# 64 latent tokens leave the dense expert path for the gathered one; V computed with tokens moving

## The chip, the cores and the metric

One core of a Trainium2 chip runs the program. The time is device microseconds from launch to end. The program is one fully unrolled stream per engine: TensorE (PE, with weight loads PEld), VectorE (DVE), ScalarE (ACT), GpSimd (POOL), and SyncE (SP), which only issues DMAs. DMAs of SP, ACT and POOL share 16 DMA engines.

## What is computed

Two layers over five tiles of 128 tokens: four tiles of latents (512 tokens) and one tile of prompt. A layer has a mixer (four head groups between an input and an output projection) and a retrieval of experts (PEER), both modulated by shifts, scales and gates from a conditioning vector, both closed by a layer norm. The change is in PEER:

```python
sv, si = lax.top_k(sc, 16)                            # 8 heads, 2 halves, 128 keys each
cand = sv[:, :, 0, :, None] + sv[:, :, 1, None, :]    # 16 x 16 sums a head
cv, ci = lax.top_k(cand.reshape(nt, 8, 256), 16)
idx, gate = i1 * 128 + i2, softmax(cv)                # 128 experts of 16384 a token
act = gelu(einsum('thkd,td->thk', u_tab[idx], x))
out = einsum('thk,thkd->td', gate * act, v_tab[idx])
```

## The kernel before

**Two ways through PEER.** The 128 prompt tokens take the *gathered path*: for each of a token's 128 experts one indirect DMA brings 128 rows of 4 KB (one per token, 512 KB), and one DVE instruction makes a dot with the token's hidden row (`gather_u`, line 1047) or adds the row, weighted, to an accumulator (`gather_v`, line 1055). That is 128 + 128 gathers a layer. The 512 latents take the *dense path*: all 16384 experts against all latents, in 128 chunks of 128 experts, with a gate matrix that is zero where a token did not choose the expert.

**U** (`a_chunk`, line 1030). A chunk of 512 KB is loaded on SP's queue, split into a high and a low float32r half (ACT copies, DVE subtracts; POOL in the first 12 chunks), and 24 matmuls of 512 columns (experts stationary, latents moving) make [128 experts, 512 tokens] in one PSUM bank. ACT applies gelu, and the ACT queue writes the block to DRAM (`gad`). Between chunks come the gathers of the prompt, the choice of 16 of 256 candidates (`pick`, line 960: one `top16` of five DVE instructions a head) and `build_gate` (line 991): per latent tile 16 steps, each two one-hot and two product tiles on DVE, 16 small f16 matmuls and two ACT copies, written to DRAM (`Gd`) by the ACT queue. The layer's main loop (lines 1222 to 1236) asks for one gather a chunk and spreads the gate's steps over chunks 4 to 108.

**V** (`v_phase`, line 1069). For a chunk, `prep` loads the hidden block (256 KB), every fourth chunk a gate tile (1 MB), and 512 KB of the second table; DVE multiplies hidden by gate, ACT and DVE split product and table into halves, and then `steps` yields one gather (two on every sixteenth chunk) and, in layer 0, `mods` one modulation block on every second chunk from 6 on. `use` makes 24 matmuls: for each of four token tiles six of 512 columns, product stationary, table moving, so that [tokens, 1024] grows in two PSUM banks a tile and all eight banks are taken:

```python
mm(p0, w[:, 0, ns], vh[:, h0], a, False)
mm(q0, w[:, 0, ns], vh[:, h1], a, False)
```

The last three chunks (`TAIL`) run tile by tile in an order written out by hand, and `close_layer` (line 1137: gate, residual, layer norm, in layer 0 also the next layer's norm and transposes) follows each tile as it is done, under the matmuls of the next.

**Modulation.** A layer's 48 blocks of 128 are dots of weight rows with the conditioning vectors, two DVE instructions a block (`mod_block`, `dot_mod`). Layer 0 makes its own in the opening, its mixers (`late_mods`, blocks 16 to 32), its routing (`route_mods`, 32 to 40) and the end of U (40 to 48); all 48 of layer 1 stand in layer 0's V.

**Order of the work.** Dependencies are tracked by tile. A planner that estimates each instruction's time orders the instructions of every engine, except where an order is written by hand; engines and queues then run in that order. `issue_after` puts instructions behind a given one. Buffers: four for gathered rows, in U two of them in idle residual tiles; ten split halves, six hidden blocks, two gate tiles.

Of the kernel before, what the change touches and what calls it, by code (L numbers as in the profile page):

```python
# [73 lines left out]
XLAST = 120  # L74
CS = 32 ** -0.5


def build(tc, nc, I, O, dbg=None):
# [311 lines left out]
    def late_mods(P, o3):  # L390
# [7 lines left out]
        for b in range(16, MID):  # L398
            pt = P.tile([128, 2, 2], F32, name="mp", bufs=4)
            for i in range(2):  # L400
                c = slice(i * 512, (i + 1) * 512)
                w = P.tile([128, 640], F32, name="e", bufs=EB)[:, :512]
                load(w, I["wmodT"][0, b, :, c])
# [8 lines left out]
            V.tensor_add(modT[0][:, :, b:b + 1], pt[:, :, 0:1], pt[:, :, 1:2])  # L412
            finish_mod(0, b, b + 1, modT[0][:, :, b:b + 1])
# [40 lines left out]
    def mixers(l, P, acc, w):  # L454
# [112 lines left out]
        mods = late_mods(P, o3) if l == 0 else iter(())  # L567
# [300 lines left out]
    def out_and_route(l, P, hn, sv, si):  # L868
# [7 lines left out]
        def norm2(n):  # L876
            post_norm(P, n, [part[:, n, 0:1], part[:, n, 1:2]], lg, lb, part[:, n, 2:3])
            k4 = [P.tile([128, D], F32, name="k4", bufs=3) for _ in range(2)]
            normalise(n, k4[0], part[:, n, 2:3])
            nc.scalar.dma_start(xm[l][n], xs[n])  # L880
            modulate_T(n, l, 24, 32, k4[0], (p1(), p1()), k4[1])
            hf_ = k4[1].rearrange("p (a b) -> p a b", a=8)
            if n == PT:
                ps = p2()
                for k in range(8):
                    T.transpose(ps[:, k * 128:(k + 1) * 128], hf_[:, k, :], ident)
                S.activation(hn, ps, AF.Copy)

        def route_mods():
# [6 lines left out]
            for b in range(MID, 40):  # L896
                t = P.tile([128, 4, 2, 128], F32, name="sc", bufs=3).rearrange("p a b c -> p (a b c)")
                load(t, I["wmodT"][0, b])
                dot_mod(t, 0, b, sB, P.tile([128, D], BF16, name="jk", bufs=1))
                yield  # L900

        mods = route_mods() if l == 0 else iter(())
# [57 lines left out]
    def pick(P, n, sv, si, i1, i2, gt):  # L960
# [4 lines left out]
        cand = P.tile([128, 8, 16, 16], F32, name="cand", bufs=1)  # L965
        G.tensor_tensor(cand, sv[:, :, 0, :, None].to_broadcast([128, 8, 16, 16]),
                        sv[:, :, 1, None, :].to_broadcast([128, 8, 16, 16]), OP.add)
        for h in range(8):
            top16(cand[:, h].rearrange("p a b -> p (a b)"), cv[:, h, :], ci[:, h, :])
# [3 lines left out]
        V.tensor_single_scalar(ab[:, 1], ci, 15, OP.bitwise_and)  # L973
        abf = P.tile([128, 2, 8, 16], F32, name="abf", bufs=1)
        V.tensor_copy(abf, ab)
        for j, dst in ((0, i1), (1, i2)):
# [14 lines left out]
    def build_gate(P, n, Gd, i1, i2, gt):  # L991
# [3 lines left out]
        i16 = P.tile([128, 2, 128], F16, name="i16", bufs=2)  # L995
        V.tensor_copy(i16, ps[:, :256].rearrange("p (a b) -> p a b", a=2))
        gT = P.tile([128, 2, 128], F32, name="gT", bufs=1)
        g16 = P.tile([128, 2, 128], F16, name="g16", bufs=2)
# [10 lines left out]
        for u in range(4):  # L1009
# [20 lines left out]
    def a_chunk(Q, l, c):  # L1030
# [7 lines left out]
        for k in range(8):  # L1038
            ks = slice(k * 128, (k + 1) * 128)
            mm(ps, uh[:, ks], Hhi[:, k, 0:512], k == 0, False)  # L1040
            mm(ps, uh[:, ks], Hlo[:, k, 0:512], False, False)
            mm(ps, ul[:, ks], Hhi[:, k, 0:512], False, k == 7)
        ga = Q.tile([128, 512], F32, name="ga", bufs=2)
        S.activation(ga, ps, AF.Gelu_apprx_tanh)  # L1044
        return ga

    def gather_u(P, l, idx, hn, dots):
        for k in range(128):
            t = P.tile([128, D], F32, name="gth", bufs=2) if k % 4 < 2 else x_tile(3 + k % 2)
            G.indirect_dma_start(out=t, out_offset=None, in_=I["u"],  # L1050
                                 in_offset=bass.IndirectOffsetOnAxis(ap=idx[:, k:k + 1], axis=0))
            V.scalar_tensor_tensor(t, t, 1.0, hn, op0=OP.mult, op1=OP.mult, accum_out=dots[:, k:k + 1])  # L1052
            yield

    def gather_v(P, l, idx, gt, dots, accp):
        bufs = GV
        S.activation(dots, dots, AF.Gelu_apprx_tanh)
        V.tensor_mul(dots, dots, gt)
        for k in range(128):
            t = P.tile([128, D], F32, name="gth", bufs=bufs)  # L1060
            G.indirect_dma_start(out=t, out_offset=None, in_=I["v"],  # L1061
                                 in_offset=bass.IndirectOffsetOnAxis(ap=idx[:, k:k + 1], axis=0))
            if k == 0:
                V.tensor_scalar(accp, t, dots[:, 0:1], None, op0=OP.mult)
            else:
                V.scalar_tensor_tensor(accp, t, dots[:, k:k + 1], accp, op0=OP.mult, op1=OP.add)  # L1066
            yield

    def v_phase(l, P, pv, Gd, gad, steps, mods, finish):
        ws, gt, lows = {}, {}, []  # L1070

        def load_gate(g):
            gt[g] = P.tile([128, 16, GLD, 32], F32, name="gate", bufs=2)
# [3 lines left out]
        def prep(c):  # L1077
            ga = P.tile([128, 512], F32, name="gr", bufs=6)
# [8 lines left out]
            w = P.tile([128, 2, 512], F32R, name="whl", bufs=4)  # L1087
# [13 lines left out]
        def use(c, n):  # L1101
            w, vh, vl = ws[c]
            ns = slice(n * 128, (n + 1) * 128)
            p0, q0 = pv[n]
            a, z = c == 0, c == NCH - 1
            h0, h1 = slice(0, 512), slice(512, 1024)
            mm(p0, w[:, 0, ns], vh[:, h0], a, False)
            mm(q0, w[:, 0, ns], vh[:, h1], a, False)
            mm(p0, w[:, 0, ns], vl[:, h0], False, False)
            mm(q0, w[:, 0, ns], vl[:, h1], False, False)  # L1110
            mm(p0, w[:, 1, ns], vh[:, h0], False, z)
            mm(q0, w[:, 1, ns], vh[:, h1], False, z)
# [5 lines left out]
        for c in range(NCH - TAIL):  # L1118
# [3 lines left out]
            for n in range(NL):  # L1122
                use(c, n)
# [6 lines left out]
        with tc.manual_schedule(engines={E.PE, E.DVE, E.Activation, E.Pool}):  # L1130
            for i in range(NL + 2):
                for n in {0: (0,), 1: (1,), 2: (2, 3)}.get(i, ()):
                    for c in range(NCH - TAIL, NCH):
                        use(c, n)
                finish(i)

    def close_layer(l, P, n, f, g2, lg, lb):
        t = P.tile([128, D], F32, name="wm", bufs=2)
        if len(f) == 2:
            for h in range(2):  # L1140
                hs = slice(h * 512, (h + 1) * 512)
                V.tensor_mul(t[:, hs], f[h], g2[:, hs])
        else:
            V.tensor_mul(t, f[0], g2)
        yield
        V.scalar_tensor_tensor(xs[n], xs[n], ALPHA, t, op0=OP.mult, op1=OP.add, accum_out=xsum[:, n, 0:1])
        c = sum_coefs(xs[n], [xsum[:, n, 0:1]], P.tile([128, D], BF16, name="jk", bufs=1))
# [14 lines left out]
    for l in range(DEPTH):  # L1162
# [8 lines left out]
        with tc.tile_pool(name=f"q{l}", bufs=1) as Q:  # L1171
            accp = Q.tile([128, D], F32, name="accp")
            A = tc.alloc_tile_pool(name=f"a{l}", bufs=1)
            hn = A.tile([128, D], F32, name="hn")
            gp = Q.tile([128, 128], F32, name="gp")
# [3 lines left out]
            Gd = dram.tile([16, 2, 128, 64 * 32], F32, name=f"Gd{l}")  # L1179
            gad = [dram.tile([128, 512], F32, name=f"gad{l}_{c}") for c in range(NCH)]  # L1180
            with tc.tile_pool(name=f"t{l}", bufs=1) as TP:
# [4 lines left out]
                with tc.tile_pool(name=f"r{l}", bufs=1) as R:  # L1186
                    out_and_route(l, R, hn, sv, si)
                with tc.tile_pool(name=f"tt{l}", bufs=1) as R:
# [12 lines left out]
                    def gates():  # L1201
                        for n in range(NL):
                            nxt = start_pick(n + 1) if n < NL - 1 else iter(())
# [7 lines left out]
                    for n in (PT, 0):  # L1211
# [8 lines left out]
                    steps = gather_u(A, l, idx, hn, dots)  # L1220
                    bg = gates()
                    for c in range(ASPLIT):
                        nc.scalar.dma_start(gad[c], a_chunk(A, l, c))
                        with tc.issue_after(pace[0].ins):
                            next(steps, None)
                        if c >= T0:
                            for _ in range((c + 1 - T0) * 64 // (T1 - T0) - (c - T0) * 64 // (T1 - T0)):
                                next(bg, None)
                    for _ in bg:
                        pass  # L1230
# [140 lines left out]
```

## Time and profile before

| | us |
|---|---|
| median of 3 runs | 4023.82 (4019.87 to 4028.7) |
| profiled execution | 4019.37 |
| its span | 4017.6 |
| PE busy | 3791.2 (94%) |
| DVE busy | 3068.7 (76%) |
| ACT busy | 1435.9 (36%) |
| POOL busy | 1218.5 (30%) |
| moved by DMA | 934.02 MB, 232 GB/s |

Busy time is the union of an engine's instructions. A matmul's end is modelled and matmuls overlap, so PE's pace is better read from the distance of their starts. The DMA share is the mean busy share of 16 engines. The shares of the whole span hide that the stages differ; the rows below are taken by stage.

### The profile page before, as it was taken

Reading aid. Unit: us, or ns where it says so; the run is one execution under the profiler, and the core shown is the slowest. Engines: PE = TensorE matmul, PEld = TensorE weight load, DVE = VectorE, ACT = ScalarE, POOL = GpSimd, SP = SyncE. Lnnn points to the kernel's source line nnn. Section 1 sums busy time; section 2 is a strip of 40 time slices with the busy share of each in tenths; the row PEclk is TensorE's granted clock in tenths of the full one; section 3 lists DMA queues with packets and bytes.
Section 4 is the critical chain, followed back from the end, with each engine's and each line's share of the span. In section 5 each row is a group of like instructions: output and inputs, shape, how many; then the busy total and the mean of one; then the engine's idle time right before and its main releaser. Section 6 shows DMA issues by size and latency. Waiting matters only on the chain. (4 is left out here: it accounts for less than half of the span.)

```text
span 4017.6 us, 52309 instructions
## 1 busy us (share of the span) xinstructions
PE 3791.2 (94%) x18606; PEld 3091.6 (77%) x18606; DVE 3068.7 (76%) x5984; ACT 1435.9 (36%) x2201; POOL 1218.5 (30%) x946
## 2 busy tenths in 40 slices
PE   6799999999999799999999999999999979999998
PEld 5577777777888688888877778777788868888886
DVE  6867799999766588988765659999986537778545
ACT  5443532333333222222344553323343322222222
POOL 5412445442111222322141243553211113343100
PEclk7899999999999899999999999999999989999999
DMA  6223248777888899999831132677788869999763
GB/s 224 79 71 118 84 139 280 251 256 272 292 263 299 298 350 346 342 343 344 261 103 52 58 106 91 237 262 246 243 307 275 263 223 341 348 340 345 251 195 104
DMA packets 405623, 934.02 MB, mean 232 GB/s; under 512 B 32624, under 2 KB 166896, under 8 KB 397168
## 3 DMA queue, kind: packets, MB, share of 16 engines
q1 hardware_dynamic: 280656, 517.34, 39.4%
q0 software_dynamic: 73728, 268.47, 19.0%
q10 hardware_dynamic: 50976, 144.87, 9.7%
q8 instruction: 146, 2.39, 0.2%
q14 instruction: 117, 0.96, 0.1%
HBM read 785.06 MB, written 145.49 MB: 232 GB/s over the span
## 5 line engine op out<-in xcount | busy, mean ns | idle before, releaser
L83 PE MATMUL pa<-Hhi,hl 128*128 128x512 f32 x4096 | 1318.7, 400 | 11.6 <-ACT ga L1044 11.5
L83 PE MATMUL p<-hl,whl 128*128 128x512 f32 x4608 | 1089.3, 390 | 0.0
L83 PEld LDWEIGHTS p<-hl,whl 128*128 128x128 f32 x4608 | 867.5, 188 | 180.3
L83 PEld LDWEIGHTS pa<-Hhi,hl 128*128 128x128 f32 x4096 | 778.9, 191 | 181.5 <-ACT ga L1044 13.9
L83 PE MATMUL pa<-Hlo,hl 128*128 128x512 f32 x2048 | 815.0, 398 | 0.0
L199 ACT ACTIVATE hl<-x 128x1024 fp32r<-128x1024 f32 x284 | 301.3, 1061 | 960.2 <-PE p L83 578.1
L1061 POOL DMA_INDIRECT gth<-v,idx x256 | 361.0, 1410 | 825.2 <-DVE accp L1066 593.6
L199 ACT ACTIVATE hl<-raw 128x1024 fp32r<-128x1024 f32 x292 | 309.0, 1059 | 775.5 <-PE pa L83 373.7
L200 DVE TENSOR_TENSOR hl<-x,hl 128x1024 fp32r<-128x1024 f32 x272 | 345.3, 1270 | 265.6 <-ACT hl L199 260.6
L200 DVE TENSOR_TENSOR hl<-raw,hl 128x1024 fp32r<-128x1024 f32 x246 | 331.2, 1347 | 238.3 <-ACT hl L199 236.2
L83 PEld LDWEIGHTS pa<-Hlo,hl 128*128 128x128 f32 x2048 | 391.3, 191 | 81.5
L83 PE MATMUL pa<-hl,Hhi 128*128 128x512 f32 x1232 | 438.5, 424 | 7.6 <-DVE gtmp L914 2.8
L83 PE MATMUL pa<-hl,whl 128*128 128x512 f32 x1536 | 391.7, 390 | 43.5 <-DMA gr<-gad 22.6
L83 PEld LDWEIGHTS pa<-hl,whl 128*128 128x128 f32 x1536 | 289.2, 188 | 104.2 <-issue 23.0
L1066 DVE SCALAR_TENSOR_TENSOR accp<-gth,dots,accp 128x1024 f32<-128x1024 f32 x254 | 325.3, 1281 | 4.5 <-DMA gth<-v,idx 2.7
L1050 POOL DMA_INDIRECT gth<-u,idx x128 | 165.9, 1296 | 462.9 <-DVE gth L1052 404.9
L1050 POOL DMA_INDIRECT x<-u,idx x128 | 168.9, 1320 | 448.7 <-DVE x L1052 425.6
L83 PEld LDWEIGHTS pa<-hl,Hhi 128*128 128x128 f32 x1232 | 235.4, 196 | 54.9 <-DVE gtmp L914 3.7
L83 PE MATMUL pa<-hl,Hlo 128*128 128x512 f32 x616 | 260.6, 423 | 14.3 <-POOL Hlo L200 10.5
L1006 DVE TENSOR_TENSOR M<-E,g 128x1024 f16<-128x1024 f16 x256 | 189.3, 771 | 58.7 <-PE p L83 57.7
L1024 ACT ACTIVATE stg<-p 128x512 f32<-128x512 f32 x256 | 138.9, 597 | 233.8 <-PE p L83 153.2
L1085 DVE TENSOR_TENSOR gr<-gr,gate 128x512 f32<-128x512 f32 x256 | 175.2, 685 | 24.7 <-DMA gate<-Gd 24.7
(339 smaller groups left out, 4635.6 us busy)
## 6 DMA issues: line engine op xcount, KB each, us to landing
x<-v SPq DMA_DIRECT2D x158, 512.0 KB
raw<-uT SPq DMA_DIRECT2D x130, 512.0 KB
gad<-ga ACTq DMA_DIRECT2D x256, 256.0 KB
Gd<-stg ACTq DMA_DIRECT2D x64, 1024.0 KB
gr<-gad SPq DMA_DIRECT2D x256, 256.0 KB
gate<-Gd SPq DMA_DIRECT2D x64, 1024.0 KB
x<-uT SPq DMA_DIRECT2D x126, 512.0 KB
raw<-v SPq DMA_DIRECT2D x98, 512.0 KB
```

Source lines behind the costliest of these rows:

```text
L83: return T.matmul(out, l, r, start=start, stop=stop, skip_group_check=True)
L199: S.activation(hi, src, AF.Copy)
L200: return (eng or V).tensor_sub(lo, src, hi.bitcast(F32))
L1006: V.tensor_tensor(out, src, col.rearrange("p (q r) -> p q r", r=2)[:, :, None, :].to_broadcast(shape), op)
L1024: S.activation(st[a][:, :, b * 8:(b + 1) * 8], v[:, a], AF.Copy, scale=1.0 / GSCALE)
L1050: G.indirect_dma_start(out=t, out_offset=None, in_=I["u"], in_offset=bass.IndirectOffsetOnAxis(ap=idx[:, k:k + 1], axis=0))
L1061: G.indirect_dma_start(out=t, out_offset=None, in_=I["v"], in_offset=bass.IndirectOffsetOnAxis(ap=idx[:, k:k + 1], axis=0))
L1066: V.scalar_tensor_tensor(accp, t, dots[:, k:k + 1], accp, op0=OP.mult, op1=OP.add)
L1085: V.tensor_mul(ga.rearrange("p (u t) -> p u t", t=32), ga.rearrange("p (u t) -> p u t", t=32), gt[c // GLD][:, :, c % GLD, :])
```

## The change

A tile of latents is cut: the last 64 tokens of tile 3 (`GS`; `R0` = 64 is their first row in the tile) join the gathered path, and the dense path keeps `DN` = 448.

- *Gathered path.* The 64 tokens' 128 experts are laid out as 128 rows by 64 columns (`PARTS` = 2 halves of 64 on the partitions), so they add 64 gathers to U and 64 to V, ahead of the prompt's. Index and gate slices go over the ACT queue into `idx2` and `gp2`; the hidden rows of the tokens are turned in routing, written to `hxd` and loaded twice into `hn2`. In V, the second half's sums are moved by one DMA and added. U asks for 192 gathers over 128 chunks, V for 194 steps over 118 chunks.
- *Dense path.* U's matmuls, gelu, hidden block, gate product and its halves have 448 columns; tile 3 has 8 gate steps instead of 16. Tiles are taken in the order 3, 0, 1, 2.
- *V turned round.* A chunk's table halves are stationary by blocks of 128 columns, the product moves: eight blocks of three matmuls with 448 columns, one PSUM bank a block. At the layer's end each block is scaled by the gate's column into `fT`, and each tile is turned back by eight transposes before it closes.
- *Pick.* Of 256 candidate sums a head, 112 are kept (first four keys with all 16, the other 12 with four), on two POOL instructions; a few small instructions recover the index pair.
- *Modulation.* Layer 1 makes blocks 16 to 48 where layer 0 makes them; layer 0's V keeps 16 of its blocks, one on every sixth chunk.
- *Buffers.* Hidden blocks and gate tiles move to a pool opened before U's last 16 chunks.

The core of the diff:

```diff
+TILES = (3, 0, 1, 2)
+GS = 64
+PARTS = 128 // GS
+R0 = 128 - GS
+DN = 512 - GS
+VEND = 118
+VSTEPS = 128 + GS + PARTS
@@ a_chunk
+            mm(ps[:, :DN], uh[:, ks], Hhi[:, k, :DN], k == 0, False)
...
@@ gather_u
+        for idx, hn, dots, cols in groups:
+            for k in range(cols):
+                t = P.tile([128, D], F32, name="gth", bufs=2) if g % 4 < 2 else x_tile(3 + g % 2)
...
@@ gather_v
+            if cols == GS:
+                for j in range(PARTS - 1):
+                    t = P.tile([128, D], F32, name="gth", bufs=GV)
+                    nc.scalar.dma_start(t[R0:], acc[j * GS:(j + 1) * GS])
+                    V.tensor_add(acc[R0:], acc[R0:], t[R0:])
+                    yield
+                V.tensor_mul(acc[R0:], acc[R0:], g2[R0:])
@@ v_phase
-                next(steps, None)
-                if c % 16 == 15:
+                for _ in range(2 * (c == 0) + (c + 1) * VSTEPS // VEND - c * VSTEPS // VEND):
                     next(steps, None)
-                if c >= MOD0 and (c - MOD0) % 2 == 0:
+                if c >= MOD0 and (c - MOD0) % 6 == 0:
                     next(mods, None)
+        def use(c, b):
+            mm(pv[b], vh[:, bs], w[:, 0], c == 0, False)
+            mm(pv[b], vh[:, bs], w[:, 1], False, False)
+            mm(pv[b], vl[:, bs], w[:, 0], False, c == NCH - 1)
...
+            for b in range(8):
+                for c in range(NCH - TAIL, NCH):
+                    use(c, b)
...
+                if b % 2:
+                    V.tensor_scalar(fT[b], pv[b], g, None, op0=OP.mult)
+                else:
+                    S.activation(fT[b], pv[b], AF.Copy, scale=g)
             for i in range(NL + 2):
                 finish(i)
@@ close_layer
+            for b in range(8):
+                o = f[b * len(f) // 8][:m, b * 128 % (1024 // len(f)):][:, :128]
+                T.transpose(o, fT[b][:, n * 128:n * 128 + m], ident)
@@ build_gate
-        for u in range(4):
+        for u in range(R0 // 32 if n == NL - 1 else 4):
@@ pick
-        cand = P.tile([128, 8, 16, 16], F32, name="cand", bufs=1)
+        cand = P.tile([128, 8, 256], F32, name="cand", bufs=1)[:, :, :112]
+        for a0, a1, nb in ((0, 4, 16), (4, 16, 4)):
...
@@ main loop
-                        next(steps, None)
+                            for _ in range((c + 1) * (128 + GS) // NCH - c * (128 + GS) // NCH):
+                                next(steps, None)
...
+            H = tc.alloc_tile_pool(name=f"h{l}", bufs=1, side="right")
             with tc.tile_pool(name=f"ta{l}", bufs=1) as R:
-                mods = mod_steps(R, [(0, b) for b in range(40, 48)], 4) if l == 0 else iter(())
+                mods = mod_steps(R, [(l, b) for b in range(40, 48)], 2)
...
-                        mod_steps(R, [(1, b) for b in range(48)], 2) if l == 0 else iter(()), finish)
+                        mod_steps(R, [(1, b) for b in range(16)], 2) if l == 0 else iter(()), finish)
```

## Rows read from the trace of the kernel before

**Rows 1.** By stage: us, PE, PEld, DVE, ACT, POOL busy, clock, DMA, GB/s.
```profile
512.00:1329.00 817.00, 781.66 (x4094) 633.18 (x4092) 683.22 (x1318) 288.44 (x409) 259.44 (x150) 0.98 0.74 254
1329.00:1350.70 21.70, 0.58 (x2) 0.51 (x3) 2.72 (x5) 3.65 (x4) 4.68 (x5) 0.56 0.97 311
1350.70:2049.50 698.80, 698.80 (x3079) 578.66 (x3078) 589.24 (x792) 209.95 (x271) 188.99 (x135) 1.00 0.92 319
2049.50:2306.00 256.50, 240.55 (x1373) 193.29 (x1372) 158.02 (x406) 131.07 (x286) 78.14 (x126) 0.97 0.20 65
2306.00:2466.00 160.00, 154.31 (x722) 126.19 (x721) 110.39 (x489) 74.72 (x111) 64.57 (x42) 0.98 0.31 98
2466.00:3283.40 817.40, 784.85 (x4103) 635.86 (x4101) 670.48 (x1292) 282.79 (x404) 249.24 (x150) 0.98 0.73 248
...
3304.00:4002.00 698.00, 697.82 (x3071) 577.50 (x3069) 476.47 (x530) 200.39 (x256) 176.42 (x130) 1.00 0.83 280
```

**Rows 2.** Chain of waits, V of layer 1: start us, us, what.
```profile
3720.31 4.08 PE p L83 x18
3725.75 4.08 PE p L83 x18
```

**Rows 3.** Busy time in two stretches of U of layer 0.
```profile
700.00:900.00 200.00, 184.88 (x958) 147.71 (x958) 200.00 (x361) 70.18 (x100) 82.19 (x42) 0.97 0.73 248
...
1200.00:1329.00 129.00, 127.51 (x588) 104.03 (x587) 69.22 (x103) 44.42 (x57) 18.65 (x15) 1.00 0.75 265
```

**Rows 4.** Timeline, mixers of layer 0: start us, us, engine, line.
```profile
145.52 0.42 PEld L83 LDWEIGHTS p<-x,x 96*128 96x128 f32 x2
145.75 0.45 PE L83 MATMUL p<-x,x 96*128 96x320 f32 x2
...
146.04 0.40 PE L83 MATMUL pa<-hl,Hhi 128*128 128x512 f32 x1
```

**Rows 5.** Groups by form, V of layer 1: busy us, mean ns, idle.
```profile
L1066 DVE SCALAR_TENSOR_TENSOR accp<-gth,dots,accp 128x1024 f32<-128x1024 f32 x99 | 126.8, 1281 | 3.9 <-DMA gth<-v,idx 2.7
L200 DVE TENSOR_TENSOR hl<-x,hl 128x1024 fp32r<-128x1024 f32 x41 | 50.2, 1225 | 39.2 <-ACT hl L199 39.0
...
L1085 DVE TENSOR_TENSOR gr<-gr,gate 128x512 f32<-128x512 f32 x65 | 44.5, 685 | 0.0
```

**Rows 6.** Groups by form, whole span.
```profile
L1006 DVE TENSOR_TENSOR M<-E,g 128x1024 f16<-128x1024 f16 x256 | 189.3, 771 | 58.7 <-PE p L83 57.7
...
L410 DVE SCALAR_TENSOR_TENSOR o<-e,o 128x512 bf16<-128x512 f32 x48 | 36.5, 761 | 3.2 <-DMA e<-wmodT 3.1
...
L418 DVE SCALAR_TENSOR_TENSOR jk<-sc,k 128x1024 bf16<-128x1024 f32 x16 | 19.5, 1220 | 3.1 <-DMA sc<-wmodT 3.1
```

**Rows 7.** DMA view, 3400 to 3650: packets, MB, share of engines; issues.
```profile
q1 hardware_dynamic: 36013, 47.87, 56.5%
q0 software_dynamic: 10279, 37.43, 39.9%
...
gth<-v,idx POOLq DMA_INDIRECT x73
```

**Rows 8.** Line 954: count, ns min/median/max, first, last start.
```profile
L954 DVE MAX8 sv<-sc x160: 274/331/584, 453.4 to 2497.6; 128x8 f32<-128x128 f32 x160
L954 DVE MAX8 cv<-cand x80: 401/406/425, 550.7 to 2812.0; 128x8 f32<-128x256 f32 x80
```

**Rows 9.** Chain of waits, hole of layer 1.
```profile
3285.97 15.38 DMA gate<-Gd
```

**Rows 10.** Timeline, end of layer 1.
```profile
3989.42 12.40 PE L83 MATMUL p<-hl,whl 128*128 128x512 f32 x54
...
4010.77 0.08 DVE L1151 DVE_READ_ACCUMULATOR x<-wm,cf,rowb 128x1 f32 x1
```

**Rows 11.** Waits, 3400 to 3650: us, times, longest.
```profile
POOL gth L1061 <- DVE accp L1066: 140.8, 49, 8.8
...
DVE accp L1066 <- DMA gth<-v,idx: 2.7, 4, 1.2
```

More of the change, by code (lines that the diff above doesn't have):

```diff
@@ L887, in norm2 @@
                 S.activation(hn, ps, AF.Copy)
+            if n == NL - 1:
+                ps = p2()
+                for k in range(8):
+                    T.transpose(ps[:, k * 128:(k + 1) * 128], hf_[:, k, :], ident)
+                hx = P.tile([128, D], F32, name="k4", bufs=3)
+                S.activation(hx, ps, AF.Copy)
+                nc.scalar.dma_start(hxd, hx[R0:])
         def route_mods():
@@ L1039, in a_chunk @@
             ks = slice(k * 128, (k + 1) * 128)
[L1040 to L1044, printed above, removed]
-        return ga
[L1047 to L1067, printed above, removed]
@@ L1070, in v_phase @@
+    def v_phase(l, P, H, pv, fT, Gd, gad, steps, mods, finish):
         ws, gt, lows = {}, {}, []
         def load_gate(g):
-            gt[g] = P.tile([128, 16, GLD, 32], F32, name="gate", bufs=2)
+            gt[g] = H.tile([128, DN // 32, GLD, 32], F32, name="gate", bufs=2)
             cc = g * GLD % 64
@@ L1201, in gates @@
                     def gates():
-                        for n in range(NL):
-                            nxt = start_pick(n + 1) if n < NL - 1 else iter(())
+                        for i, n in enumerate(TILES):
+                            nxt = start_pick(TILES[i + 1]) if i < NL - 1 else iter(())
                             for _ in build_gate(R, n, Gd, i1[n], i2[n], gt[n]):
@@ L1219, in build @@
                             show(n)
-                    steps = gather_u(A, l, idx, hn, dots)
+                        else:
+                            idf = R.tile([128, 128], F32, name="sif", bufs=1)
+                            V.scalar_tensor_tensor(idf, i1[n], 128.0, i2[n], op0=OP.mult, op1=OP.add)
+                            V.tensor_scalar(idf, idf, float(l * 16384), None, op0=OP.add)
+                            idr = R.tile([128, 128], I32, name="ab", bufs=1)
+                            V.tensor_copy(idr, idf)
+                            for j in range(PARTS):
+                                ps_, cs_ = slice(j * GS, (j + 1) * GS), slice(j * GS, (j + 1) * GS)
+                                nc.scalar.dma_start(idx2[ps_], idr[R0:, cs_])
+                                nc.scalar.dma_start(gp2[ps_], gt[n][R0:, cs_])
+                    hn2 = R.tile([128, D], F32, name="hn2")
+                    for j in range(PARTS):
+                        load(hn2[j * GS:(j + 1) * GS], hxd)
+                    steps = gather_u(A, l, ((idx2, hn2, dots2, GS), (idx, hn, dots, 128)))
                     bg = gates()
@@ L1235, in build @@
                     with tc.issue_after(pace[0].ins):
-                        next(steps, None)
+                        for _ in range((c + 1) * (128 + GS) // NCH - c * (128 + GS) // NCH):
+                            next(steps, None)
                     next(mods, None)
@@ L1243, in build @@
                 wide = [p2(), p2()]
-                pv = [(pacc(), pacc()), (p1(), p1())] + [(t[:, :512], t[:, 512:]) for t in wide]
+                pv = [t[:, h * 512:h * 512 + DN] for t in wide for h in range(2)]
+                pv += [t[:, :DN] for t in (p1(), p1(), pacc(), pacc())]
+                acc2 = R.tile([128, D], F32, name="acc2")
+                fT = []
                 if dbg and "f" in dbg:
```

140 lines of the change are left out of this document (90 added, 50 removed).

## The prediction

> **What bounds the kernel now.** The first view to read is the table by stage [rows 1]. A layer is a mixer and routing part, then U (chunks of the first expert table against the latents), a hole, and V (the gated chunks back to tokens). U takes 817 us a layer, V 698; the four together are 3031 of the 4017.6 us, with PE busy 96% of U and all of V. [...] So V is PE's. What the reader is to see beside it: DVE is busy 589 of 699 us in layer 0's V, and the DMA engines 0.92 and 0.83 of the two V stages. In U, DVE is busy 200.0 of 200 us at 700 to 900, and PE is nearly full later, 127.5 of 129 at 1200 to 1329 [rows 3]: DVE sets the pace first, PE at the end.
>
> **The change, part by part.**
>
> *Columns.* Each of the 3072 matmuls of a U stage, and of a V stage, moves 448 columns instead of 512. Is a shorter matmul quicker, when each has a weight load shown as 0.21 us? Two neighbouring 320-column matmuls, each with its load, start at 145.75, and the next matmul at 146.04: 145 ns each [rows 4]. So the load is hidden. (226.7 - 145) / 192 is 0.4255 ns a column, and 448 columns cost 199.5 ns. PE saves 27.2 ns x 3072 = 84 us in each of the four stages, if nothing else is late. A V chunk needs 24 x 199.5 ns = 4.79 us of PE, U 782 - 84 = 698 us (its gate matmuls left whole, though an eighth goes).
>
> *V, on DVE.* By chunk: the gate product, and the low half of it that takes as long, shrink by an eighth from 0.685 to 0.60 each; the low half of the table stays 1.225; gathers come at 194 steps over 118 chunks, 1.64 x 1.281 = 2.10 [rows 5]. Sum 4.53 us, under PE's 4.79. In layer 0 a modulation block, two dots of 1.22 us [rows 6] and some small work, 2.8 together, follows every sixth chunk, 0.47 a chunk: 5.0, a little over PE. Before, 48 such blocks stood there, now 16.
>
> *V, transfers.* The DMA view of 3400 to 3650 has 56.5% of 250 us for the loads of 46 chunks (250 / 5.44), 3.07 us of all 16 engines a chunk, and 39.9% for 73 gathers, 1.366 us each [rows 7]. The gate and the hidden block, half of a chunk's bytes, shrink by an eighth: 2.88. With 1.64 gathers: 2.88 + 2.24 = 5.12 us a chunk. This is the term that decides: for 118 chunks the transfers become the longest, over PE's 4.79, where before 3.07 + 1.07 x 1.366 = 4.53 stood under PE's 5.44. In layer 1 I take 5.15: 118 x 5.15 + 10 x 4.79 = 656 us against 698, **-42**. In layer 0 the 16 blocks load 512 KB each, as a gather does, and DVE is nearer: 5.30, so 673, **-26**. Bounds for each stage: 613 (128 x 4.79, PE's alone) and 698 plus some 30, if DVE, whose instructions go in order, stands behind late gathers.
>
> [...]
>
> *U.* DVE's 683 us [rows 1] change so. 64 more dots of 1.22 and a read: +83. Of 64 gate steps 8 go, each four instructions of 0.77 [rows 6]: -25. The candidates shrink from 256 columns to 112; the maximum over 256 takes 0.406, over 128 at best 0.274 [rows 8], so 40 heads x 5 instructions x 0.13 = -26. Index arithmetic in five picks and one more index tile: +12. Together +44: 727. Transfers: 0.74 x 817 = 605, and 64 gathers x 1.366: 692 (the ACT queue's smaller writes left out). So three resources stand at 698, 727 and 692. Before, the stage took 817 for PE's 782, 4.5% over its longest. With three so close I take 7% over the longest: 778, **-39** a layer, -78. Bounds: 727 (DVE never idle, -90) and 840 (+23, if the backlog of 700 to 900 grows and PE stands behind it). The eight modulation blocks that the end of layer 1's U gets, 22 us, find DVE idle 60 of 129 us there [rows 3].
>
> *The hole.* Between U and V PE stands still for 21.7 us in layer 0 [rows 1] (20.6 in layer 1), and the chain is there on the gate's load, 15.38 us [rows 9]. Gate and hidden block move to a pool of their own, opened before U's last 16 chunks, so their loads can start under U. Next late are the product, its split and the chunk's own split, 5 to 8 us by DVE's rows. I take **-28** for both; bounds 0 and -42.
>
> *Layer 1 gets modulation work.* 16 blocks in its mixers (36.5 us of DVE in layer 0's) and 8 in its routing (19.5) [rows 6]. DVE is 62% busy in those mixers and 69% in that routing, PE 94 and 96% [rows 1]; some hides. Between 0 and +56 I take **+26**, near the middle since both are near full by turns. The transfers there are at 0.20 and 0.31, which hides the loads.
>
> *The layer's end.* The last 72 matmuls stay, but no tile can close before all eight blocks are done; then come 32 transposes and four closings. Before, closings ran under the last 54 matmuls, and DVE ended 9 us after PE [rows 10]. After, four closings of some 4.1 us (1.22, two of 1.28, 0.3 of small work) and 2 us of scaling and turning stand behind PE, 19 in all: **+11** a layer, +22; bounds 0 and +40. In layer 0 the prompt's projection can fill a part.
>
> *Queues.* The new ACT-queue transfers (index and gate slices, the hidden rows, one partial sum), one more tile turned in routing: each stands once a layer behind work of that queue, **+4**, bounds 0 and +15. POOL is busy 189 of 699 us, which hides 64 more gather issues a stage; its longer wait is in the transfers' term.
>
> *Sum*, on the profiled execution's own 4019.4 us (span 4017.6): -42 - 26 - 78 - 28 + 26 + 22 + 4 = -122, 3897. The median of the runs is 4.4 us longer than that execution, so 3902 in their terms.
>
> **Rivals.**
> 1. *The transfers don't bind V.* For it: in the window of 96% DVE waited for a gather only 2.7 us [rows 11], so that share need not be a limit yet. Against: 5.12 us of transfers would have to fit in 4.8. V is then 617 in layer 1 and 640 in layer 0 (DVE): -81 and -59, in all -194, 3825, or 3830 in the runs' terms. Chance 0.25.
> 2. *The gathers become the bound, and it is slower.* A V gather has four buffers and went at 250 / 73 = 3.42 us, with POOL standing 140.8 us until DVE had freed one [rows 7, 11]. At that pace 192 take 657 us; from about 3.8 us a gather on (V and U 730) the kernel is slower. At 4.0, with the transfers full and DVE waiting in order, V and U take 768: +140 - 98 - 28 + 52 = +66, 4090. Against it: POOL waited for DVE's turn, not for landings. 0.13.
> 3. *Hardly a gain.* U stays at 817 as DVE's backlog meets more gathers, and layer 1's modulation is bare: -68 - 28 + 56 + 26 = -14, 4010. 0.10.
> 4. *The matmuls get no shorter*, held by their loads: 4071 with the added work. [Rows 4] leave it 0.01.
>
> **How the numbers follow.** The forecast has 0.51, with 3850 to 3965 as its own range. Rival 1 lies below, the others above. Leaving out most of rival 2, the upper part of 3 and the far side of 1, the range is 3805 to 4000. A measurement of this kernel tells about 0.2%, 8 us. Faster are the forecast, rival 1 and half of rival 3: 0.81; slower rivals 2 and 4: 0.14; the same 0.05.
>
> **What would show it.** Chunks in V 5.1 to 5.3 us apart with a DMA share near 1: the forecast; 4.8: rival 1; over 5.7: rival 2. A 448-column matmul 199 to 200 ns after the one before. U about 780 with DVE over 90% busy. A hole under 10 us. Layer 1's mixers and routing about 26 us longer. Some 19 us from PE's last large matmul to DVE's end. The prediction is wrong if V's chunks come at PE's 4.8 us, or if U doesn't shorten.

## The result, and the profile after

The changed kernel takes 3983.88 us (median of 4 runs, 3969.79 to 3992.55) against 4021.85 (4 runs, 4019.75 to 4028.7). The ratio is 0.990, 95% interval 0.986 to 0.994. That is 38 us faster where the prediction's sum had 122: the direction held, the size did not. The profiled execution is the longest of the four, 3992.55 us with a span of 3990.8, 26.8 us under the 4017.6 of before; the sums below are made against that span.

The table by stage of the changed kernel, layer 0 and then layer 1. Columns are as in [rows 1]: stretch, its us, busy us of PE, PEld, DVE, ACT and POOL with instructions, the granted clock, the DMA share, GB/s.

```profile
508.00:1259.80 751.80, 697.07 (x3990) 633.42 (x3988) 699.22 (x1459) 275.37 (x394) 336.47 (x212) 0.97 0.85 308
1259.80:1282.40 22.60, 0.04 (x1) 0.00 (x0) 14.53 (x24) 1.97 (x4) 11.22 (x9) 0.57 0.78 263
1282.40:1906.20 623.80, 623.74 (x3009) 566.38 (x3009) 497.84 (x609) 195.53 (x256) 177.14 (x145) 1.00 0.96 332
1906.20:2002.80 96.60, 0.36 (x3) 0.09 (x1) 61.97 (x49) 0.63 (x1) 61.83 (x50) 0.53 0.82 273
2002.80:2018.70 15.90, 15.18 (x65) 13.52 (x66) 10.96 (x15) 5.60 (x9) 1.51 (x4) 0.87 0.17 65
2018.70:2320.00 301.30, 247.28 (x1379) 196.76 (x1378) 213.38 (x554) 146.69 (x326) 106.52 (x147) 0.92 0.27 89
2320.00:2495.00 175.00, 159.69 (x743) 129.41 (x742) 131.83 (x511) 80.88 (x117) 66.55 (x43) 0.96 0.36 116
2495.00:3248.40 753.40, 694.21 (x3993) 630.24 (x3991) 700.47 (x1464) 276.90 (x395) 334.44 (x213) 0.97 0.85 308
3248.40:3270.00 21.60, 0.00 (x0) 0.00 (x0) 14.20 (x24) 0.63 (x2) 10.30 (x8) 0.52 0.77 262
3270.00:3893.30 623.30, 623.25 (x3009) 565.96 (x3009) 483.05 (x541) 190.21 (x251) 180.09 (x164) 1.00 0.96 330
3893.30:3948.70 55.40, 0.30 (x2) 0.00 (x0) 35.98 (x29) 0.63 (x1) 36.50 (x29) 0.54 0.85 278
3948.70:3964.70 16.00, 15.27 (x65) 13.54 (x66) 10.83 (x14) 3.15 (x5) 0.77 (x2) 0.88 0.19 74
3964.70:3990.80 26.10, 3.67 (x32) 3.17 (x30) 17.76 (x31) 4.97 (x8) 2.96 (x8) 0.66 0.20 80
```

Read it against [rows 1]. U fell by 65 and 64 us, and its DVE is busy 93% of the stage. The holes stayed. V has a stretch that it did not have: PE runs without a gap for 624 and 623 us, then stands still for 96.6 and 55.4 us while DVE and POOL work off 49 and 29 more gathers, and only then does the rest of its matmuls, 16 us. V is so 736 us in layer 0 (before 699) and 695 in layer 1 (before 698). The waits in PE's idle stretch of layer 1 (who, for whom; us, times, longest):

```profile
ACT gth L1170 <- DVE accp L1094: 60.6, 1, 60.6
...
PE p L90 <- ACT gth L1170: 55.1, 1, 55.1
DVE accp L1094 <- DMA gth<-v,idx: 19.8, 24, 1.6
```

PE waits for ACT, which wants to write a scaled block of the result (fT) into a tile "gth", the gather buffers' name; that buffer is free only after the last gathers. So the last 63 matmuls, which needed nothing from the gathers, stood behind the drain (the stretch in which the left-over gathers are worked off).

The DMA view of 3400 to 3650, as [rows 7]:

```profile
DMA packets 46478, 82.39 MB, mean 330 GB/s; under 512 B 2816, under 2 KB 32081, under 8 KB 46461
...
q1 hardware_dynamic: 37493, 49.57, 59.7%
q0 software_dynamic: 8888, 32.35, 35.8%
...
gth<-v,idx POOLq DMA_INDIRECT x63
```

The kernel asks for 1.64 gathers a chunk and gets 63 in 50.4 chunks (250 us at 4.96), 1.25. The bytes agree: 330 GB/s times 4.96 us is 1.64 MB a chunk; table, gate and hidden block are 0.52 + 0.23 + 0.23 = 0.98; the remaining 0.65 MB are 1.25 gathers of 0.524 MB. This is bookkeeping: it comes out whatever held the gathers back. Two theories stood here. T: transfers are full, the loads for PE's chunks take what PE's pace asks, gathers get the rest. P: four gather buffers and the order of the adds on DVE hold the gathers back, and the transfers only look full. For P spoke the waits: POOL stood for DVE to free a buffer,

```profile
POOL gth L1089 <- DVE acc L1094: 98.5, 31, 7.8
POOL gth L1089 <- DVE accp L1094: 74.1, 24, 6.7
```

as in [rows 11], while DVE seldom waited for a landing. In all of layer 1's chunks, 3270 to 3893.3, it was 6.7 us:

```profile
DVE acc L1092 <- DMA gth<-v,idx: 5.7, 1, 5.7
DVE acc L1094 <- DMA gth<-v,idx: 1.0, 1, 1.0
```

The expectations below take the order of the adds as the source asks for it, all gathers by chunk 118. The built order is another one. DVE takes its instructions in the order that the planner gave them, so the trace shows it. Line 1094, which makes 190 of a layer's 192 adds, in the chunks and in PE's idle stretch of layer 0, then of layer 1 (stretch, its us, DVE's busy us on that line with instructions, clock, DMA share, GB/s):

```profile
1282.40:1906.20 623.80, 177.75 (x139) 1.00 0.96 332
1906.20:2002.80 96.60, 61.97 (x49) 0.53 0.82 273
3270.00:3893.30 623.30, 203.27 (x159) 1.00 0.96 330
3893.30:3948.70 55.40, 35.98 (x29) 0.54 0.85 278
```

So 51 and 31 of these adds are ordered behind the chunks, whether or not their gathers could have come earlier. Each run below was planned anew, and what it says of T and P depends on what became of this order.

### The profile page after: what moved, and what is told of

It is laid out like the page before. It is cut to its first block, busy times and chain, and to the rows that moved or that the text cites. A ratio compares the mean times of both kernels' runs of the same rounds, so it can differ in the third digit from the quotient of the medians.

```text
span 3990.8 us, 53144 instructions
## 1 busy us (share of the span) xinstructions
PE 3504.2 (88%) x18430; PEld 3093.0 (78%) x18430; DVE 3255.1 (82%) x6422; ACT 1424.3 (36%) x2223; POOL 1518.6 (38%) x1228
## 5 line engine op out<-in xcount | busy, mean ns | idle before, releaser
L90 PE MATMUL pa<-Hhi,hl 128*128 128x448 f32 x4096 | 1204.0, 371 | 30.1 <-ACT ga L1068 30.1
L90 PE MATMUL p<-whl,hl 128*128 128x448 f32 x4608 | 1000.8, 370 | 198.4 <-ACT gth L1170 152.8
L90 PEld LDWEIGHTS p<-whl,hl 128*128 128x128 f32 x4608 | 870.0, 189 | 288.4 <-ACT gth L1170 154.3
L90 PE MATMUL pa<-Hlo,hl 128*128 128x448 f32 x2048 | 756.6, 369 | 0.0
L1077 POOL DMA_INDIRECT gth<-u,idx x192 | 267.1, 1391 | 388.4 <-DVE gth L1079 296.7
L90 PE MATMUL pa<-whl,hl 128*128 128x448 f32 x1536 | 359.1, 369 | 0.0
L90 PEld LDWEIGHTS pa<-whl,hl 128*128 128x128 f32 x1536 | 288.9, 188 | 29.2
L1079 DVE SCALAR_TENSOR_TENSOR x<-x,hn 128x1024 f32<-128x1024 f32 x192 | 260.4, 1361 | 18.5 <-DMA x<-u,idx 18.2
L1079 DVE SCALAR_TENSOR_TENSOR gth<-gth,hn 128x1024 f32<-128x1024 f32 x192 | 234.2, 1226 | 17.4 <-DMA gth<-u,idx 16.1
L207 POOL TENSOR_TENSOR hl<-raw,hl 128x1024 fp32r<-128x1024 f32 x46 | 121.1, 2644 | 171.0 <-ACT hl L206 170.8
```

The costliest lines, as they stand in the source:

```text
L90: return T.matmul(out, l, r, start=start, stop=stop, skip_group_check=True)
L207: return (eng or V).tensor_sub(lo, src, hi.bitcast(F32))
L1077: G.indirect_dma_start(out=t, out_offset=None, in_=I["u"], in_offset=bass.IndirectOffsetOnAxis(ap=idx[:, k:k + 1], axis=0))
```

## The experiments

All are against the changed kernel (3984 us) unless another base is named; times are medians. Executions of one kernel differ by 9 to 35 us, in part perhaps for what the last section tells, so stages are compared before sums.

**1. Scaled blocks elsewhere.** Five later runs contain it.

```diff
-                if b % 2 == 0:
-                    pair = P.tile([128, 2, DN], F32, name="gth", bufs=GV)
-                fT.append(pair[:, b % 2])
+                if b % 4 == 0:
+                    four = H.tile([128, DN // 32, GLD, 32], F32, name="gate", bufs=2)
+                    four = four.rearrange("p u c t -> p (u c t)")
+                fT.append(four[:, b % 4 * DN:(b % 4 + 1) * DN])
```

> One change to the changed kernel: the scaled blocks of the result (fT) lie in the two gate buffers, which are free by then, and no longer in the gather buffers. Nothing else. Theory A (the last 63 matmuls of a layer stand behind the drain only because fT shares the gather buffers): TensorE runs the last 63 matmuls right after the last chunk, under the drain of gathers; the 13 us of these matmuls leave the end of each layer, about -26 us for the kernel: 3955 to 3965 us against 3984. Theory B (the end of the layer waits for the gathers' sum anyway, and the blocks' transposes too): the matmuls move, the end of the drain stays where it is, 0 to -10 us.

3966.48 us (3956.88 to 3975.05), 17 less. PE's last matmuls now run at 1895 to 1910 us, ahead of the drain. Between the two theories of its expectation: the matmuls left the end, and of the 32 us that they stood there (16 a layer) about half came back as time. That half is rough: the ranges overlap, and run 9, the same program as the changed kernel, had a median of 3976.

**2. Another layout of the gated weights.** `[128, 2, DN]` becomes `[128, 2, 512]`, cut to DN; gr buffers 6 to 5.

> One change to the changed kernel: the weight buffer of V (whl) is laid out with 512 columns a row instead of 448, of which 448 are used, so that the low part begins at a multiple of 2048 bytes as U's operand does; to make room one of six gr buffers goes. Theory A (the layout makes V's 448-column matmuls 206.7 ns apart where U's are about 200): they fall to 199.5 to 202 ns, V's chunks from 4.96 to 4.8 us, -14 to -22 us a layer in the chunk loop; the kernel gains that only as far as the drain of gathers does not take it back, 3945 to 3984 us. Theory B (the spacing comes from the weight loads, 188 ns each here, or from the row of three matmuls on one bank, not from where the operand lies): 206.7 ns stays, 3975 to 3995 us.

3989.19 us (3983.36 to 3997.82), V's matmuls 206.6 ns apart: the layout is not the cause. One gr buffer less costs little: the medians differ by 5 us, inside the spread.

**3. Without the second set of gathers in V.**

```diff
-            for k in range(cols):
+            for k in range(1 if cols == GS else cols):
...
-VSTEPS = 128 + GS + PARTS
+VSTEPS = 128 + 1 + PARTS
```

> Of the 64 gathers that V does for the 64 joined latent tokens only the first is left in (63 gathers of 512 KB and their adds are left out a layer, 126 in all; the output of those tokens lacks them). Theory P (the order of the adds and the four buffers hold the gathers back) and theory T (the transfers are full) both expect the drain behind the chunks to go: 96 us less idle TensorE in layer 0 and 55 us in layer 1, V with its chunks at 4.96 us or a little less, 3825 to 3850 us. The share of time in which the transfers run tells them apart a little: T expects it to fall to about .85 with gathers landing in 6 to 7 us still, P expects the issue-to-add time of 13 us to stay. A third theory (the drain is the cost of something else, such as the planner's handling of the closing steps) expects 3930 us or more.

3835.66 us (3814.65 to 3845.51): 148 less, the two drains (152) by their size. V's 3009 matmuls still take 623 us in each layer, and PE's loads had thus not been held up by gathers. Layer 1 shows it best: 32 adds of line 1094 fewer in its chunks, a DMA share of 0.88 instead of 0.96, and the same pace. Both theories expected the drains to go; the share, which T had put at about .85, was 0.93 and 0.88:

```profile
1275.30:1898.50 623.20, 623.15 (x3009) 565.97 (x3009) 488.42 (x606) 198.94 (x261) 150.96 (x135) 1.00 0.93 322
3161.10:3785.00 623.90, 623.90 (x3008) 566.61 (x3009) 448.51 (x516) 191.26 (x253) 147.80 (x131) 1.00 0.88 303
```

**4. Without most gate loads.** Meant to tell T from P.

```diff
         def load_gate(g):
+            if g > 1:
+                gt[g] = gt[g - 1]
+                return
```

> The gate loads of V are left out but for the first two groups of four chunks (some 28 MB less to load in each V, wrong gates from the ninth chunk on); all else is as in the changed kernel. Theory T (transfers are full in V, .96 of the time, so the gathers come late): 28 MB of some 227 MB are 12%, 75 to 85 us of transfer a layer; the drain shrinks by 50 to 96 us in layer 0 and goes in layer 1 (55 us): 3840 to 3890 us. Theory P (the order of the adds and four buffers hold the gathers back, the transfers only look full): the drain stays within 15 us a layer, 3960 to 3990 us.

3820.51 us (3815.77 to 3832.57), 163 less, more than T expected (3840 to 3890) and far from P's 3960 to 3990. All gathers come within the chunks. V's chunks of layers 0 and 1, and the stretch behind those of layer 0, where PE goes straight on:

```profile
1282.30:1905.50 623.20, 623.17 (x3009) 565.99 (x3009) 557.87 (x659) 195.42 (x256) 263.62 (x194) 1.00 0.93 330
1905.50:1921.00 15.50, 14.05 (x71) 12.40 (x70) 10.92 (x15) 6.37 (x10) 3.80 (x5) 1.00 0.20 73
3168.90:3780.50 611.60, 611.57 (x3008) 566.81 (x3009) 524.19 (x579) 191.31 (x253) 274.49 (x194) 1.00 0.89 319
```

POOL, whose work in V's chunks is nearly all gathers (144 of 145 instructions in layer 0 of the changed kernel, all 164 in layer 1), ran 194 instructions inside the chunks of each layer where it had run those 145 and 164. But the run changed two things at once: with less to load, the planner also built another order. Line 1094 in the two chunk stretches, where the changed kernel has 139 and 159:

```profile
1282.30:1905.50 623.20, 241.60 (x189) 1.00 0.93 330
3168.90:3780.50 611.60, 243.19 (x190) 1.00 0.89 319
```

So the run shows that both drains go, 152 us by their size, when some 28 MB a layer need not be loaded (12 us more are layer 1's quicker matmuls, see the last section). It does not show whether the transfers or the order had held the gathers, and P is not refuted by it.

**5. Modulation back in V of layer 0.** `late_mods`, `route_mods` and layer 1's last eight blocks for layer 0 only; V of layer 0 makes 48 blocks, one each second chunk.

> The changed kernel with one part undone: all 48 modulation blocks of layer 1 are made in V of layer 0 again (one every second chunk), none in layer 1's mixers, routing and U. Theory T (V is held by its transfers, as the run without gate loads showed): layer 1's mixers and routing fall by 40 to 60 us (from about 476 to 420 to 435), and V of layer 0 grows by what 32 blocks of 512 KB take of full transfers, 17 MB at 334 GB/s, 50 us; net -15 to +20 us, 3970 to 4000. Rival (the move was simply a loss, as the prediction priced V's modulation at what DVE has left there): layer 1 gains the 40 to 60 us and V of layer 0 grows by under 15: 3930 to 3955 us.

3984.96 us (3975.86 to 3987.36): no difference, as T expected. It does not single out T, for the built order is another one: 108 adds of line 1094 in layer 0's chunks, not 139. PE's idle stretch in V of layer 0 grows to 156 us (V 796 us, +60):

```profile
1908.00:2070.00 162.00, 5.89 (x18) 5.04 (x17) 107.42 (x82) 0.64 (x1) 99.79 (x81) 0.52 0.80 266
```

From V's last matmul to the end of layer 1's first U chunk it is 435 us instead of 482, and from there to V 760 instead of 770: 56 us less. The move of the modulation saved 60 us at one place and cost 56 at the other.

**6. 256 candidates in a pick again.** `pick` as before the change, all else as after.

> The changed kernel with one part undone: the candidates of a pick are all 256 sums again and not 112 (the same 16 best come out), with the shorter index arithmetic that belongs to it. Theory U1 (VectorE sets U's length; U fell more than forecast because VectorE has 700 us of work there and not 727): U grows by about what the maxima cost, 40 heads a layer times five instructions of some 0.13 to 0.2 us each less the index arithmetic of 10 us, so +15 to +30 us a layer, 4010 to 4040 us. Theory U2 (TensorE sets U's length, 697 of 752 us, and VectorE's work is hidden): U changes by less than 8 us a layer, 3975 to 4000 us.

4029.27 us (10 runs, 4014.05 to 4049.08), +45. U of both layers:

```profile
510.00:1289.00 779.00, 699.05 (x3994) 633.72 (x3992) 732.62 (x1439) 277.00 (x395) 347.33 (x207) 0.95 0.83 298
...
2521.00:3298.00 777.00, 697.23 (x3997) 632.48 (x3995) 733.29 (x1444) 276.90 (x395) 347.46 (x209) 0.96 0.84 300
```

DVE's busy time grows by 33 us a layer and U by 27 and 24, with PE's the same. DVE's work now sets most of U's length; without the shorter candidate list the change would not have been faster at all.

**7. Gated weights early** (on 1): two of four whl buffers come from the pool opened under U, `w = (H if c % 4 < 2 else P).tile(..., bufs=2)`.

> The run with the scaled blocks in the gate buffers, and one thing more: two of the four buffers for V's gated weights (whl) lie in the pool that is opened before U's last chunks, and not in memory that U's gathers free. Theory A (the hole between U and V, 22.6 and 21.6 us, is the wait for that memory): the first gated weights are made under U's end, the hole falls to 5 to 9 us in both layers, and V starts 14 us earlier in each; since V ends with its transfers, which start earlier too, the kernel gains 15 to 28 us over that run: 3938 to 3952 us. Theory B (what is late next, the hidden block's or the chunk's load, or the last dots of U that VectorE has before it, keeps the hole): 18 us or more of it stay and the time is 3955 to 3975 us.

3953.93 us (3948.22 to 3959.86), 13 under run 1, with ranges that overlap. The holes are gone: V's first matmul starts at 1252.3, under U's last ones, and PE is busy 24 of the 30 us in which it stood still for 22.

```profile
1252.30:1283.00 30.70, 24.16 (x121) 22.30 (x119) 19.63 (x28) 7.02 (x9) 15.05 (x13) 0.93 0.91 322
1283.00:1904.90 621.90, 612.91 (x3030) 570.18 (x3031) 506.23 (x620) 197.87 (x260) 203.47 (x151) 0.99 0.96 337
1904.90:1996.70 91.80, 0.70 (x5) 0.27 (x3) 64.42 (x53) 1.28 (x2) 54.10 (x44) 0.53 0.81 277
```

But the last gather is added at 1996.7, where run 1 had it at 1999.8: the 24 us that PE had gained came back as a longer V, in layer 1 too (3925.0 and 3925.9). V's gathers need U's dots and started no earlier: the first add began at 1300.9, in run 1 at 1294.8. The hole was the wait for memory that U's gathers free, not for the gate's load; in the changed kernel's hole of layer 0 ACT's first whl stood behind the dots of U:

```profile
ACT whl L206 <- DVE x L1079: 20.6, 1, 20.6
```

Closing it hardly pays while the gathers end V.

**8. 32 tokens instead of 64** (on 7): `GS = 32`, so 480 columns; gr buffers 6 to 5.

> As the run before (scaled blocks in gate buffers, two gated weight buffers early), but 32 latent tokens join the gathered path instead of 64: 480 columns move, 160 gathers a stage (one of six gr buffers goes to make room). Theory T: V moves 214 MB instead of 227, at 334 GB/s 640 us; 3072 matmuls of 480 columns at 213 to 220 ns take 654 to 676, so the chunks cover the transfers and no drain is left: V with its last matmuls 665 to 685 in both layers instead of about 730 and 685. U gets 13 ns a matmul back, 41 us of TensorE, and loses 35 us of VectorE's dots: 750 to 780 instead of 752. In all 3905 to 3975 us. If the gathers are held by buffers and order rather than by transfers, a drain of 30 us or more stays in layer 0 and the time is above 3975.

3948.58 us (3938.03 to 3952.0). No drain is left in either layer; V is PE's again, as T expected:

```profile
1310.00:1968.50 658.50, 656.82 (x3031) 568.27 (x3030) 536.60 (x632) 201.92 (x260) 224.12 (x163) 1.00 0.95 332
2444.00:3245.00 801.00, 759.40 (x4097) 642.98 (x4095) 693.00 (x1449) 287.27 (x409) 301.51 (x190) 0.98 0.81 284
3245.00:3905.80 660.80, 659.30 (x3043) 570.41 (x3042) 497.35 (x545) 194.56 (x253) 216.75 (x161) 1.00 0.90 314
```

U pays for it, some 800 us where 750 to 780 were expected, with PE at 95%. The planner built another order here too: all adds of line 1094 stand ahead of the last 63 matmuls. Layer 1 has a DMA share of 0.90.

**9. Gathers asked for earlier.** `VEND = 118` becomes 98.

> The changed kernel with one number changed: V asks for all its gathers by chunk 98 instead of 118 (1.98 a chunk instead of 1.64). Theory T (chunk loads take what TensorE's pace asks, the gathers get what is left of the transfers, about 1.25 a chunk): nothing changes, the drain stays at 85 to 110 us in layer 0 and 45 to 65 in layer 1, 3970 to 3995 us. Theory P (the place of the adds in the order sets when a buffer comes free): the drain shrinks by 20 to 60 us a layer, 3880 to 3950 us.

3976.06 us (3966.41 to 3993.54); PE idle for 95 and 54 us. In 450 us of layer 1's V, taken from 30 us after its start, 116 gathers are issued, in the changed kernel 114. That is no test of P, for the edit changed nothing that runs: every engine executes the same instructions in the same order as in the changed kernel. Line 1094 in the two chunk stretches:

```profile
1283.80:1895.30 611.50, 177.84 (x139) 1.00 0.97 338
3257.30:3868.60 611.30, 202.81 (x159) 1.00 0.96 336
```

As a second execution of the same program it tells more. PE's matmuls came quicker (last section), so the chunks took 12 us less a layer. The same bytes went at 338 and 336 GB/s instead of 332 and 330, and PE's idle stretches stayed as long (94.7 and 54.4 us against 96.6 and 55.4). Transfers that were full at 332 would not have done that, and if gathers only got what was left over, shorter chunks would have left more of them for the end. In the chunks of the changed kernel the built order held the gathers, then: P, with the planner and not the source setting the order. Why the planner sets it so is open.

What the transfers would bear is not shown. Layer 1's V needs 125.8 MB for 128 chunks of 0.983 and 100.7 for its 192 gathers, 226.5 in all (222.4 of it moved between 3270 and 3965 us of the changed kernel). In 128 chunks of 4.96 us that would be 357 GB/s (an estimate). The most that a chunk stretch shown here moved is 343, at a DMA share of 0.96 (run 10); at a share of 0.99 it was 340 (run 12). No run has an order that asks 357 of them with all loads in place.

**10. Five gather buffers** (on 7): `GV = 5`, gr buffers 6 to 4.

> As the run with the scaled blocks in gate buffers and two gated weight buffers early, with five gather buffers instead of four (two of six gr buffers go to make room). Theory T: in the chunk loop nothing changes, 1.25 gathers a chunk; in the drain, where four buffers go round at some 1.9 us a gather and transfers run only .76 to .82 of the time, five bring 1.6 us a gather, 10 to 17 us less in layer 0 and 6 to 10 in layer 1: 3928 to 3942 us against 3954. Theory P (buffers hold the gathers back in the whole of V): a quarter more gathers in the chunk loop, the drain of both layers goes: 3830 to 3900 us. If the gr buffers are what V misses, chunks come over 5 us apart and the time is over 3955.

3927.16 us (3921.9 to 3932.34), 27 under run 7, 1 us past T's range. In 450 us of layer 1's chunks 117 gathers are issued, hardly more than before. The drains are shorter, at higher rates (chunks and drain of layer 0, then of layer 1):

```profile
1300.00:1907.50 607.50, 590.95 (x2902) 545.70 (x2901) 507.23 (x609) 192.85 (x244) 209.05 (x154) 0.99 0.96 343
1922.70:1975.40 52.70, 1.10 (x9) 0.68 (x6) 43.43 (x36) 1.69 (x2) 30.83 (x26) 0.55 0.85 307
3240.00:3840.10 600.10, 599.38 (x2949) 552.55 (x2947) 477.89 (x530) 191.62 (x243) 239.14 (x161) 1.00 0.98 338
3851.00:3891.20 40.20, 3.35 (x29) 2.85 (x27) 32.20 (x27) 0.00 (x0) 26.66 (x21) 0.57 0.83 286
```

In layer 0's chunks they did bring more, 142 gathers from 1312 to 1872 where run 7 has 128 and the changed kernel 125. The built order tells why there: line 1094 from V's first matmul to the last 63 of layer 0, run 7 and then this run,

```profile
1252.30:1889.30 637.00, 174.70 (x137) 0.99 0.97 338
1252.10:1907.50 655.40, 199.24 (x155) 0.99 0.96 343
```

and in layer 1 156 and 158. In layer 0's chunks PE was idle for 17 us (591 busy of 607.5); that the two gr buffers given up are the cause is likely, but not shown.

**11. 32 tokens in layer 0, 64 in layer 1** (on 7): `GS = (32, 64)[l]`, and what follows from it, set at each layer's start.

> As the run with scaled blocks in gate buffers and two gated weight buffers early, but with 32 tokens in the gathered path in layer 0, whose V has modulation blocks to load too, and 64 in layer 1. Theory T says that each layer is best where its chunks just cover its transfers: layer 0 as in the run of 32 tokens (layer 1's U began 32 us earlier there), layer 1 as in the run of 64 (from there on 14 us shorter), 3915 to 3930 us. If the layers are not independent (what one saves comes back in the next one's mixers), it is no better than the run with 32 in both, 3938 to 3955.

3930.33 us (5 runs, 3928.05 to 3947.5): the layers add up, just past the upper edge of what was expected.

**12. The same with five gather buffers in layer 1.**

> The run with 32 tokens in layer 0 and 64 in layer 1, with five gather buffers (and four gr buffers) in layer 1. If the drain of layer 1 is held by the number of buffers, as five of them took 15 us from it in the run before, and layer 0 is left as it was: 3912 to 3922 us. If five buffers helped only because of layer 0, 3925 to 3935.

3910.86 us (5 runs, 3906.01 to 3925.15), ratio to the kernel before 0.974 (0.973 to 0.976): the best of all, 1 us below what was expected and 9 us over what the change had been forecast to take. Layer 0 has no drain, layer 1 one of 40 us:

```profile
1310.00:1966.00 656.00, 654.32 (x3019) 566.09 (x3018) 535.93 (x631) 201.33 (x260) 223.67 (x162) 1.00 0.95 332
3240.00:3823.30 583.30, 583.30 (x2898) 543.57 (x2897) 468.31 (x521) 188.90 (x239) 225.76 (x156) 1.00 0.99 340
3838.90:3878.70 39.80, 3.35 (x29) 2.85 (x27) 32.17 (x27) 0.00 (x0) 26.27 (x21) 0.60 0.82 288
```

## Why the prediction was right and wrong

| term | forecast | in the spans |
| --- | --- | --- |
| V of layer 0 and 1 | -26, -42 | +37, -3 |
| U, both | -78 | -129 |
| holes, both | -28 | +2 |
| layer 1's mixers and routing (modulation, one layer end, queues) | +41 | +60 |
| last layer's end | +11 | +10 |
| start up to U | 0 | -4 |
| sum | -122 | -27 |

*The step that failed is V's transfers.* The prediction gave each chunk its 1.64 gathers and let it wait for their share of the transfers, 5.15 us a chunk. The runs show in place of that: the chunks never waited (4.96 us, PE's own pace), the built order had only 139 and 159 of the 190 adds in them, and the rest was worked off behind the chunks, where PE stood still for 97 and 55 us. In layer 1 the matmuls took 639 us in all, 17 less than the forecast 656, and the drain added 55: that is the miss of 39. In layer 0 it is 640 for 673, and 97: the miss of 63. Run 3, without the left-over gathers, is 148 us quicker, about the two drains. That the transfers were full in the chunks was the premise, and run 9 speaks against it. What is open is why the planner leaves these adds to the end, and whether the transfers would bear them in the chunks; at the rate of [rows 7], 85.3 MB in 250 us or 341 GB/s, layer 1's 226.5 MB would take 664 us (an estimate), near the forecast's 656.

The sign "V's chunks at PE's pace" was read as rival 1, transfers that don't bind; it came, and V was longer all the same. A chunk's pace told nothing of the gathers, because PE does not wait for them until the layer's end. Rival 2, the gathers as the bound, was nearer than its 0.13: they came every 3.97 us in the window, with POOL standing for DVE's turn. Its threshold of 3.8 is not what its own terms give, which make the kernel slower from 3.9 on (V and U 752). The kernel was faster nevertheless: behind the chunks a gather took only 1.9 to 2.0 us, so V lost 34 us in both layers and not 140, and U gave 129 where that rival had 98.

*U* was right in its rule and mis-sized in one term. DVE's busy time in layer 0 grew by 16 us, not 44 (in layer 1 by 30, with 22 for its eight modulation blocks): 11 of the 192 dots fall into the hole, as the groups of DVE in U of layer 0 show,

```profile
L1079 DVE SCALAR_TENSOR_TENSOR x<-x,hn 128x1024 f32<-128x1024 f32 x90 | 122.9, 1371 | 7.5 <-DMA x<-u,idx 7.4
L1079 DVE SCALAR_TENSOR_TENSOR gth<-gth,hn 128x1024 f32<-128x1024 f32 x91 | 111.0, 1226 | 3.6 <-DMA gth<-u,idx 3.5
```

and the five steps a head on 112 columns save 30, not 26, beside smaller pieces. The longest resource was thus 700, and the stage came out 7.5% over it, where 7% had been taken. Run 6 bears it out: 33 us more of DVE made U 27 and 24 us longer, with PE's work the same.

*The hole* failed: the gate's load was hidden as forecast, but what was late next had been missed. The whl tiles reuse memory of U's pool, and U's gathers end 20 us after its matmuls (ACT's wait for x in the hole, 20.6 us). It is the prediction's own question, what is late next, answered by duration rows and not by who holds the memory.

*Modulation in layer 1* was put in the middle of 0 and +56; run 5 gives 47 there and 10 more in U, whose eight blocks the forecast had at nothing. A DVE that is 62 and 69% busy hid little of it.

*The layer's end* (+10 for +11; by its own terms 19 less 9 is 10) and the matmul's saving held: PE's work in U is 697 us for 698 forecast. The 226.7 ns of a 512-column matmul and the 5.44 us of a chunk, with which the forecast reckons, are read from [rows 2]: 18 matmuls in 4.08 us, and the next 18 start 5.44 us later. In V the matmuls were 206.7 ns apart, not 199.5, 22 us a layer. This counts: in run 9, at 202.7, V was 14 and 13 us shorter, with the same order.

## What to carry to other kernels

Before a shared resource is called full, look for who waits for it. Here the 16 DMA engines were busy 0.96 of the time, yet PE's chunks never stood still and DVE waited for a gather for 7 us of 623, while the gathers waited for a place in DVE's order. Where a planner orders the instructions, read the order out of the trace: count how many adds lie in the chunks and how many behind them, and set that beside what the source asks. An experiment that should hold the order fixed has to be checked the same way; run 4 changed it unseen, and run 9 changed nothing at all. Leave such work no tail: choose the split so that the gathers end with the chunks (each layer has its own split in run 12), and let nothing that could run under the tail share its buffers.

## What the runs showed of the hardware

One matmul stream ran at two paces. V's matmuls stood 206.6 ns apart in the changed kernel and 202.7 in run 9, which is the same program, at a granted clock of 1.00 in both. In run 4 both paces are in one execution: its rows above show 3009 matmuls in 623 us and 3008 in 612, each without a pause. That is 12 us a layer and 24 in both; the eight runs of this program (the changed kernel and run 9) lie within 27 us. That the pace makes this spread is likely and not shown, since each run has one trace. In the kernel before V's matmuls were 226.7 ns apart in both layers and its four runs lay within 9 us. What decides the pace is open: run 2 excludes the operand's row length (206.6 with rows of 512), and with whl tiles in two pools it was 201.4 in both layers of run 7, but 203.3 in layer 1 of runs 10 and 11.
